# Gate chunks beside the inverse and the scan, latent attention behind the scan

## The chip, the core and the metric

The kernel runs on one core of one Trainium2 chip. The metric is the device time of one execution in microseconds, as a median over runs. The core has five engines that matter here, each with a queue of its own that it works off in order: TensorE (PE, with its weight loads as PEld), VectorE (DVE), ScalarE (ACT), GpSimd (POOL) and SyncE (SP, which issues most DMA transfers).

## What is computed

The reference is one block of a language model on 512 tokens of width 1024, in float32: a two-way RWKV-7 time mix (a scan with a matrix state) and a multi-head latent attention (MLA) side by side, mixed by sigmoid gates, then a mixture of single-neuron experts (PEER), and a gated input of a second kind. The part that the change touches, cut to its core:

```python
h = rmsnorm(x, g_mix)
u = h @ w_in
u_rw, u_mla = u[..., :RW_COLS], u[..., RW_COLS:RW_COLS + MLA_COLS]
gates = sigmoid(u[..., RW_COLS + MLA_COLS:]).reshape(B, T, 2, D)
y_rw = rwkv7_time_mix(u_rw, ...)
y_mla = mla_mix(u_mla, positions, ...)
merged = gates[:, :, 0] * (y_rw @ w_br_rwkv) + gates[:, :, 1] * (y_mla @ w_br_mla)
x = x + merged @ w_out
```

The time mix has 8 heads of 64, in both directions. The attention has 8 heads with 64 plain and 32 rotated (rope) dimensions for q and k, and 64 for v.

## The kernel before

Float32 products are made from two float32r parts: a weight or an input is split into a high and a low part (`whi`, `wlo`; `xh`, `xl`), and each product is three matmuls (`mm3`, L136). A projection chunk of 128 output columns (`uchunk`, L261) is 8 x 3 = 24 matmuls of 512 columns; its weights come by one DMA of 512 KB (`wload`, L121), a copy on ScalarE (L132) and a subtraction on VectorE (L133).

The order of the work is written as Python generators. `drive(main, fill)` (L99) takes a piece of `main`, which says by `yield n` how much filler may stand behind it, and then takes pieces of `fill` until their sum reaches n (in units that are meant as nanoseconds of TensorE). This gives an order of the program; a planner then builds each engine's queue from it, taking the first instruction in this order that is ready by its own estimate of times, so that later work can be pulled into holes where its buffers allow it.

The stages are:

1. `prep` (L335): for each of four pairs of heads c it projects k, r and v (`u_k`, `u_r`, `u_v`), makes decays and rates (`w_a`, for both directions d), normalises k, builds the inputs of the chunked scan (`abkr`), Gram matrices (`gram`) and transposes (`bkt_`, `v_t`), and stores them in memory as packed matrices `pk_d`; 32 pieces of them return as `U`. Beside it, as filler, run `others` (the four chunks of the latent attention's input, the rope tables) and then the first `NG` = 6 of the 16 gate chunks (`gates`, L633; `oth`, L641).
2. `inverse` (L555): 31 steps of forward substitution on VectorE, with two blocks b of 32 x 32 in separate instructions, so that a step is two products and two sums. The result goes to memory (`x_d`, `xt_d`) and comes back as `Xs` and `Xt`.
3. The rest of the gate chunks and the start of the attention stand behind the inverse in the program.
4. `chain` (L652): the scan in 8 steps, with two packed matrices `PK` in the room of `xh` and `xl`, so that it starts when the last gate chunk has read its input. Beside it, as filler, runs the attention.
5. `attn` (L818): values, then for each head `proj_q` and `proj_k`, and for each head and block of 128 queries a score (`score`), a softmax on VectorE and ScalarE, four transposes (`trans`) and the product with v (`pv`). `proj_q` rotates q of each head on 32 partitions on VectorE.
6. The end of `chain` normalises the scan's output (L784 to L811). Then both branches are projected with the gates (`wbr`), and the rest of the kernel follows.

## Time and profile before

| | us |
|---|---|
| median of 3 runs | 1916.23 (1915.2 to 1919.95) |
| the profiled execution | 1914.83 |
| its span | 1912.7 |
| TensorE busy | 1821.6 (95%) |
| VectorE busy | 1540.8 (81%) |
| ScalarE busy | 827.2 (43%) |

A group of instructions is shown as: line, engine, operation, output <- inputs, shape, count | busy us, mean ns of one | idle time of the engine just before them, and what ended it. A row of a timeline begins with the start and the duration in us; "x2" says that two instructions are merged into one row. A row of the chain of waits has the start, the us on the chain, and what it was. Durations of instructions that follow each other overlap a little, so the distance of two starts is the better price. "Clock" is the share of its full speed that TensorE was granted in a stretch.

### The profile page before, as it was taken

How to read it: one execution, taken by the hardware profiler on the slowest of the kernel's cores; microseconds unless marked ns; L12 is line 12 of the kernel's file. 1: busy time of each engine (PE TensorE's matmuls, PEld its weight loads, DVE VectorE, ACT ScalarE, POOL GpSimd, SP SyncE). 2: the span in 40 equal slices, each digit the busy share in tenths (PEclk: the TensorE clock that was granted, in tenths of full speed). 3: DMA queues.
4: the chain of work that ended last, by engine and by line, in shares of the span. 5: the costliest groups of instructions: out<-in, count | busy, mean ns of one | idle time of the engine just before them, and what ended most of it. 6: DMA issues, size and time to landing. Idle time of an engine off the chain costs nothing.

```text
span 1912.7 us, 29780 instructions
## 1 busy us (share of the span) xinstructions
PE 1821.6 (95%) x10969; PEld 1569.8 (82%) x10969; DVE 1540.8 (81%) x3103; ACT 827.2 (43%) x1224; POOL 468.4 (24%) x449
## 2 busy tenths in 40 slices
PE   7999869999999998999999999999999999999997
PEld 6777647777677888999999989888888888888775
DVE  6865778889855889999898965878788788778777
ACT  4755533666334333444444433333333333333354
POOL 1012331220101000332233021334344354344100
PEclk9999989999999999999999999999999999999999
DMA  4355664763434333889999899899999999999862
GB/s 166 90 151 174 165 179 144 226 204 105 149 105 143 100 100 100 260 289 347 339 342 327 307 354 350 315 338 340 338 335 343 322 352 340 340 327 335 280 214 99
DMA packets 196721, 470.19 MB, mean 246 GB/s; under 512 B 33312, under 2 KB 100896, under 8 KB 192736
## 3 DMA queue, kind: packets, MB, share of 16 engines
q1 hardware_dynamic: 146688, 273.23, 43.4%
q0 software_dynamic: 49744, 194.80, 28.7%
q8 instruction: 86, 1.41, 0.3%
q14 instruction: 59, 0.48, 0.1%
q10 hardware_dynamic: 144, 0.26, 0.0%
HBM read 397.97 MB, written 70.25 MB: 245 GB/s over the span
## 4 chain that ended last, share of the span: by engine, by line
PE 69%; DVE 13%; DMA 10%; issue 5%; ACT 3%; POOL 0%; SPq 0%; DVEq 0%; POOLq 0%; ACTq 0%
PE po L1498 20%; PE pa L1150 7%; PE pa L1148 7%; PE pa L1149 7%; DMA row<-in_v,e 6%; PE mm L141 3%; PE mm L142 3%; PE mm L143 3%; DVE wlo L133 2%; PE po L1377 2%; PE q L141 2%; PE q L142 2%; PE q L143 2%; DVE acc L1103 1%; DMA gt<-gates_d 1%
## 5 line engine op out<-in xcount | busy, mean ns | idle before, releaser
L132 ACT ACTIVATE whi<-wraw 128x1024 fp32r<-128x1024 f32 x352 | 370.4, 1058 | 429.7 <-PE pa L1149 157.4
L133 DVE TENSOR_TENSOR wlo<-wraw,whi 128x1024 fp32r<-128x1024 f32 x352 | 428.3, 1221 | 89.6 <-ACT whi L132 82.9
L1150 PE MATMUL pa<-hh,wlo 128*128 128x384 f32 x1024 | 348.9, 341 | 4.3 <-DVE wlo L133 4.3
L1148 PE MATMUL pa<-hh,whi 128*128 128x384 f32 x1024 | 348.9, 341 | 3.5 <-ACT gs L1156 2.5
L1149 PE MATMUL pa<-hl,whi 128*128 128x384 f32 x1024 | 348.3, 340 | 0.0
L1085 POOL DMA_INDIRECT row<-in_u,e x128 | 165.6, 1293 | 423.9 <-DVE row L1093 326.9
L1498 PE MATMUL po<-wlo,wh 128*128 128x512 f32 x768 | 239.1, 392 | 4.3 <-DVE wlo L133 4.3
L1085 POOL DMA_INDIRECT row<-in_v,e x128 | 178.5, 1395 | 248.6 <-DVE acc L1103 234.2
L1498 PE MATMUL po<-whi,wl 128*128 128x512 f32 x768 | 238.4, 392 | 0.0
L1498 PE MATMUL po<-whi,wh 128*128 128x512 f32 x768 | 211.0, 390 | 4.5 <-issue 3.4
L1103 DVE SCALAR_TENSOR_TENSOR acc<-row,pre,acc 128x1024 f32<-128x1024 f32 x127 | 162.7, 1281 | 54.8 <-DMA row<-in_v,e 54.2
L1148 PEld LDWEIGHTS pa<-hh,whi 128*128 128x128 f32 x1024 | 193.2, 189 | 8.2 <-ACT gs L1156 3.2
L1150 PEld LDWEIGHTS pa<-hh,wlo 128*128 128x128 f32 x1024 | 193.0, 189 | 6.6 <-DVE wlo L133 4.6
L1149 PEld LDWEIGHTS pa<-hl,whi 128*128 128x128 f32 x1024 | 193.0, 188 | 3.8
L1498 PEld LDWEIGHTS po<-wlo,wh 128*128 128x128 f32 x768 | 144.6, 189 | 32.4 <-DVE wlo L133 5.1
L1498 PEld LDWEIGHTS po<-whi,wl 128*128 128x128 f32 x768 | 145.3, 189 | 30.9
L1093 DVE SCALAR_TENSOR_TENSOR row<-row,h2t 128x1024 f32<-128x1024 f32 x128 | 155.4, 1220 | 17.5 <-DMA row<-in_u,e 17.4
L1498 PEld LDWEIGHTS po<-whi,wh 128*128 128x128 f32 x768 | 143.0, 188 | 29.4 <-issue 3.6
L147 ACT ACTIVATE wh<-gl 128x384 fp32r<-128x384 f32 x72 | 37.9, 526 | 214.3 <-PE po L1498 214.2
L147 ACT ACTIVATE wh<-ga 128x384 fp32r<-128x384 f32 x48 | 25.2, 524 | 128.2 <-PE po L1498 83.2
L141 PE MATMUL mm<-xh,whi 128*128 128x512 f32 x184 | 74.5, 405 | 4.9 <-ACT gt L637 3.3
L1297 ACT ACTIVATE st<-g 128x512 f32<-128x512 f32 x96 | 50.9, 600 | 54.3 <-PE g L1296 54.3
(465 smaller groups left out, 3178.7 us busy)
## 6 DMA issues: line engine op xcount, KB each, us to landing
wraw<-in_uT SPq DMA_DIRECT2D x128, 512.0 KB
wraw<-in_v SPq DMA_DIRECT2D x128, 512.0 KB
gd<-st POOLq DMA_DIRECT2D x12, 2048.0 KB, 8.2
g<-gd SPq DMA_DIRECT2D x32, 768.0 KB
wraw<-in_w_in SPq DMA_DIRECT2D x35, 512.0 KB
pk<-pk_d SPq DMA_DIRECT2D x16, 1024.0 KB
ga_d<-gs SPq DMA_DIRECT2D x72, 192.0 KB
gl<-ga_d SPq DMA_DIRECT2D x72, 192.0 KB
```

Source lines behind the costliest of these rows:

```text
L132: nc.scalar.activation(hi, raw, AF.Copy)
L133: (nc.gpsimd if s.nw <= NWP else nc.vector).tensor_sub(lo, raw, hi.bitcast(F32))
L141: nc.tensor.matmul(out, hi[:, kw], xh[:, kx], start=(i == 0), stop=False)
L142: nc.tensor.matmul(out, hi[:, kw], xl[:, kx], start=False, stop=False)
L143: nc.tensor.matmul(out, lo[:, kw], xh[:, kx], start=False, stop=(i == n - 1))
L1085: nc.gpsimd.indirect_dma_start(out=r, out_offset=None, in_=table, in_offset=bass.IndirectOffsetOnAxis(ap=e3[:, hk:hk + 1], axis=0))
L1093: nc.vector.scalar_tensor_tensor(r, r, 1.0, h2t, op0=OP.mult, op1=OP.mult, accum_out=pre[:, u:u + 1])
L1103: nc.vector.scalar_tensor_tensor(acc, r, pre[:, u:u + 1], acc, op0=OP.mult, op1=OP.add)
L1148: nc.tensor.matmul(pa, hi[:, k], hh[:, k, 0:NDT], start=(k == 0), stop=False)
L1149: nc.tensor.matmul(pa, hi[:, k], hl[:, k, 0:NDT], start=False, stop=False)
L1150: nc.tensor.matmul(pa, lo[:, k], hh[:, k, 0:NDT], start=False, stop=(k == 7))
L1498: nc.tensor.matmul(po[tb][:, half], w[:, ts], v[:, hs], start=(m == 0 and w is wh and v is vh), stop=(m == 127 and w is wl))
```

## The change

The gate chunks leave the preparation: `oth` is now only `others()`, and one generator `gates(0, 16)` serves as the filler of `inverse` and then of the scan. A gate chunk gives way after every three matmuls (680 units) instead of after the whole chunk, and the preparation gives way only at its start. In `prep` the decays for a direction are made half a turn earlier than they are used. The inverse handles both blocks b in one instruction, and yields after every third step. The scan's packed matrices get a pool of their own (`PKP`), which is released when the scan has ended; only then is the attention's pool `M` made, in part in the same room. The scan's output step is a generator of its own (`chain_out`) with the attention as filler. In the attention the columns of the query weights are laid out anew on the host, so that the rotation is made for four heads at once on 128 partitions (`proj_r`), and its 32 rows for each head are moved by DMA into place; `proj_q` makes two heads at once. `vt` moves into the room of `xh`. The transposes use another PSUM tag (`TC` = 0).

```diff
...
     qi = []
-    for h in range(8):
-        b = h * 96
-        qi += [b + i for i in range(96)] + [b + 80 + i for i in range(16)] + [b + 64 + i for i in range(16)]
+    for g in range(2):
+        bs = [h * 96 for h in range(g * 4, g * 4 + 4)]
+        qi += [b + i for b in bs for i in range(64)] + [b + 64 + i for b in bs for i in range(32)]
+        qi += [b + 64 + (i + 16) % 32 for b in bs for i in range(32)]
     A["wqup"] = c(mla_w_qup[0][:, np.array(qi)].reshape(2, 128, 2, 4, 128).transpose(2, 1, 3, 0, 4)
                   .reshape(2, 128, 8, 128))
...
         yield UNS * 2
         normalise()
         yield UNS * 2
+
+        w_a(0, 0)
         for c in range(4):
             u_k(c)
-            w_a(c, 0)
+            w_a(c, 1)
             u_r(c)
             k_norm(c)
             abkr(c, 0)
-            yield UNS
-            w_a(c, 1)
+            if c < 3:
+                w_a(c + 1, 0)
             if c:
                 gram(c - 1, 1)
                 u_v(c)
...
             if c == 2:
                 shifted(14, lg)
                 nc.scalar.activation(lg, lg, AF.Sigmoid)
-            yield UNS
             if c < 3:
                 gram(c, 0)
-                yield 100
                 bkt_(c, 0)
         gram(3, 0)
         gram(3, 1)
-        yield UNS
         for d in range(2):
             bkt_(3, d)
         v_t(3)
...
 
     def inverse():
 
-        X = [YM.tile([128, 32, 32], F32, name=f"X{b}", tag=f"ym{b}") for b in range(2)]
-        tmp = MU.tile([128, 2, 256], F32, name="xtmp", tag="gt")
+        X = YM.tile([128, 2, 32, 32], F32, name="X", tag="ym")
+        tmp = PKP.tile([128, 2, 256], F32, name="xtmp")
+        nc.gpsimd.memset(X, 0.0)
         for b in range(2):
-            (nc.vector, nc.gpsimd)[b].memset(X[b], 0.0)
+            nc.gpsimd.memset(X[:, b].rearrange("p r c -> p (r c)")[:, ::33], 1.0)
+        for k in range(31, 0, -1):
+
+            w = 32 - k
+            t = tmp[:, :, 0:k * w].rearrange("p b (r c) -> p b r c", r=k)
+            nc.vector.tensor_mul(t, U[:, :, 0:k, k:k + 1].to_broadcast([128, 2, k, w]),
+                                 X[:, :, k:k + 1, k:].to_broadcast([128, 2, k, w]))
+            nc.vector.tensor_add(X[:, :, 0:k, k:], X[:, :, 0:k, k:], t)
+            if k % 3 == 0:
+                yield YI
+        XTt = PKP.tile([128, 32, 32], F32, name="XTt")
+        nc.vector.tensor_copy(XTt, X[:, 0].rearrange("p r c -> p c r"))
         for b in range(2):
-            nc.vector.memset(X[b].rearrange("p r c -> p (r c)")[:, ::33], 1.0)
-        for k in range(31, 0, -1):
-            w = 32 - k
-            t = [tmp[:, b, 0:k * w].rearrange("p (r c) -> p r c", r=k) for b in range(2)]
-            for b in range(2):
-                nc.vector.tensor_mul(t[b], U[:, b, 0:k, k:k + 1].to_broadcast([128, k, w]),
-                                     X[b][:, k:k + 1, k:].to_broadcast([128, k, w]))
-            for b in range(2):
-                nc.vector.tensor_add(X[b][:, 0:k, k:], X[b][:, 0:k, k:], t[b])
-        XTt = M.tile([128, 32, 32], F32, name="XTt", tag="th")
-        nc.vector.tensor_copy(XTt, X[0].rearrange("p r c -> p c r"))
-        for b in range(2):
-            nc.sync.dma_start(x_d[:, b], X[b])
+            nc.sync.dma_start(x_d[:, b], X[:, b])
         nc.sync.dma_start(xt_d, XTt)
 
 
...
 
     def gates(i0, i1, tag="u", pl=None):
         for i in range(i0, i1):
-            ps = uchunk(19 + i, tag, pl)
+            hi, lo = wload(A["w_in"][19 + i], pl)
+            ps = mm_tile(tag=tag)
+            for k in range(8):
+                for w, x in ((hi, xh), (hi, xl), (lo, xh)):
+                    nc.tensor.matmul(ps, w[:, k], x[:, k], start=(k == 0 and w is hi and x is xh), stop=(k == 7 and w is lo))
+                if k < 7:
+                    yield 680
             gt = MU.tile([128, T], F32, name="gt")
             nc.scalar.activation(gt, ps, AF.Sigmoid)
             nc.sync.dma_start(gates_d[i], gt)
-            yield UNS
-
-    oth = itertools.chain(others(), gates(0, NG))
+            yield 680
+
+    oth = others()
     drive(prep(), oth)
     for _ in oth:
         pass
     s.WX.release()
     s.WX = None
     YM = pool(name="ym", bufs=1, side="right")
-    M = pool(name="mla", bufs=2, side="right")
-    GW = pool(name="gw", bufs=2)
+    CH = pool(name="ch", bufs=2)
+    PKP = pool(name="pk", bufs=1)
+    L = {}
 
 
     def chain():
...
         XS = [CH.tile([128, 8, 64], F32, name=f"Xs{i}", bufs=1) for i in range(2)]
         for x in XS:
             nc.gpsimd.memset(x, 0.0)
-        PK = [s.BIG.tile([128, 2, 2048], F32, name=f"pk{i}", tag=("xh", "xl")[i]) for i in range(2)]
+        PK = [PKP.tile([128, 2, 2048], F32, name=f"pk{i}") for i in range(2)]
...
-        L = {}
 
         def load_p(cc, i):
             nc.sync.dma_start(PK[cc % 2][:, i], pk_d[2 * cc + i])
...
+    def chain_out():
+
         g2 = CH.tile([128, 512], F32, name="g2", tag="sw", bufs=1)
         nc.gpsimd.dma_start(g2, A["g2"])
         yield 2000
...
         cql = M.tile([128, 3, T], F32R, name="cql", bufs=1)
         for i in (2, 0, 1):
             split(cqh[:, i], cql[:, i], cqn[:, i])
-        vt = M.tile([128, 4, 8, 2, 64], F32R, name="vt", bufs=1)
+        vt = s.BIG.tile([128, 4, 8, 2, 64], F32R, name="vt", tag="xh")
         for kb in range(4):
             ks = slice(kb * 128, kb * 128 + 128)
             ps = mm_tile(tag="mm")
...
                 nc.tensor.matmul(ps, x[:, 2, ks], flat(w)[:, 512:], start=(i == 0), stop=(i == 2))
             split(vt[:, kb, :, 0], vt[:, kb, :, 1], ps.rearrange("p (h v) -> p h v", h=8))
             yield 650
-        ym = [YM.tile([128, 2, T], F32, name=f"ym{b}", tag=f"ym{b}") for b in range(2)]
-        ymla.extend(ym[c // 2][:, c % 2] for c in range(4))
+        ym = YM.tile([128, 4, T], F32, name="ym", tag="ym")
+        ymla.extend(ym[:, c] for c in range(4))
         KH = [M.tile([128, T], F32R, name=f"kh{i}", bufs=1) for i in range(3)]
         KL = [M.tile([128, T], F32R, name=f"kl{i}", bufs=1) for i in range(3)]
         for i in range(3):
             nc.gpsimd.tensor_copy(KH[i][64:96], krt[64:96])
             nc.gpsimd.tensor_sub(KL[i][64:96], krt[64:96], KH[i][64:96].bitcast(F32))
         sc_ = 96.0 ** -0.5
-        Q, EU, wq, O, TH = {}, {}, [None], [None], [None]
+        Q, RH, EU, wq, O, TH = {}, {}, {}, [None], [None], [None]
+
+        def proj_r(g):
+
+            wq[0] = wload(A["wqup"][g])
+            hi, lo = wq[0]
+            pr = [mm_tile(tag="mm") for _ in range(2)]
+            for i in range(2):
+                mm3(pr[i], hi, lo, cqh, cql, [(4 + i * 2 + k, k) for k in range(2)])
+            rt = M.tile([128, T], F32, name="rt", tag="e", bufs=EB)
+            r2 = M.tile([128, T], F32, name="r2", tag="e", bufs=EB)
+            nc.vector.tensor_mul(rt, pr[0], cosT)
+            nc.vector.tensor_mul(r2, pr[1], sinT)
+            nc.vector.tensor_add(rt, rt, r2)
+            rr = MU.tile([128, 3, T], F32R, name="rr", tag="cqn", bufs=1)
+            split(rr[:, 0], rr[:, 1], rt)
+            RH[g] = rr[:, 0], rr[:, 1]
 
         def proj_q(h):
-            if h % 4 == 0:
-                wq[0] = wload(A["wqup"][h // 4])
+
             hi, lo = wq[0]
             pq = mm_tile(tag="mm")
-            mm3(pq, hi, lo, cqh, cql, [(h % 4 * 2 + k, k) for k in range(2)])
-            qh = M.tile([128, T], F32R, name="qh")
-            ql = M.tile([128, T], F32R, name="ql")
-            rt = M.tile([128, T], F32, name="rt", tag="e", bufs=EB)
-            split(qh[0:64], ql[0:64], pq[0:64])
-            nc.vector.tensor_mul(rt[64:96], pq[64:96], cosT[64:96])
-            nc.vector.tensor_mul(rt[96:128], pq[96:128], sinT[96:128])
-            nc.vector.tensor_add(rt[64:96], rt[64:96], rt[96:128])
-            split(qh[64:96], ql[64:96], rt[64:96])
-            Q[h] = qh, ql
+            mm3(pq, hi, lo, cqh, cql, [(h % 4 // 2 * 2 + k, k) for k in range(2)])
+            for i in range(2):
+                qh = M.tile([128, T], F32R, name="qh", bufs=3)
+                ql = M.tile([128, T], F32R, name="ql", bufs=3)
+                split(qh[0:64], ql[0:64], pq[i * 64:i * 64 + 64])
+                r0 = (h + i) % 4 * 32
+                for x, r in zip((qh, ql), RH[h // 4]):
+                    nc.gpsimd.dma_start(x[64:96], r[r0:r0 + 32])
+                Q[h + i] = qh, ql
 
         def proj_k(h):
             pk = mm_tile(tag="mm")
...
                 nc.scalar.activation(y, O[0][64:128], AF.Copy)
                 nc.vector.tensor_add(y, y, O[0][0:64])
 
+        proj_r(0)
         proj_k(0)
         proj_q(0)
-        yield 1950
-        if PRE:
-            yield -1
+        yield 4700
         for n in range(32 + LP):
             if n < 32:
                 if n % 4 == 1 and n < 28:
                     h = n // 4 + 1
-                    proj_q(h)
-                    yield 1300
+                    if h == 3:
+                        proj_r(1)
+                        yield 2700
                     if h % 2 == 0:
+                        proj_q(h)
                         proj_k(h)
-                        yield 650
+                        yield 2000
                 score(n)
                 yield 650
             if LT_ <= n < 32 + LT_:
...
-    inverse()
+    rest = gates(0, 16, GT)
+    drive(inverse(), rest)
     Oa = R.tile([128, 4, T], F32, name="Oa")
+    drive(chain(), rest)
+    for _ in rest:
+        pass
+    PKP.release()
+    M = pool(name="mla", bufs=2, side="right")
     rest = attn()
-    for _ in gates(NG, NG + GK, GT):
-        pass
-    if PRE:
-        while next(rest) >= 0:
-            pass
-    for _ in gates(NG + GK, 16, GT, GW):
-        pass
-    GW.release()
-    CH = pool(name="ch", bufs=2)
-    drive(chain(), rest, lambda: tc.high_priority(offset=HP) if HP else contextlib.nullcontext())
+    drive(chain_out(), rest)
     for _ in rest:
         pass
     M.release()
...
     return s
 
 
-HP = 0 
-YA = 800
-YB = 800
-YC = 800
-Y0 = 8000
+YA = 1900
+YB = 1900
+YC = 1900
+Y0 = 5000
 ZC = 0
 GQ = 0
 GT = "mm"
 EN = "a"
 NWP = 0
-TC = 99
+TC = 0
 LT_ = 2
 LP = 3
-PRE = 1
-GK = 4
-NG = 6
+YI = 4800
 EB = 3
 NEG = -3.0e38
 GS = 32768.0
```

## Rows read from the trace of the kernel before

**Rows 1.** Length, busy us of PE, PEld, DVE, ACT, POOL; clock, DMA, GB/s.

```profile
58.00:210.00 152.00, 151.10 (x738) 114.97 (x736) 107.59 (x175) 89.70 (x116) 31.18 (x41) 1.00 0.52 142
...
263.00:331.00 68.00, 55.80 (x222) 42.28 (x221) 59.71 (x158) 23.39 (x34) 6.87 (x9) 0.90 0.37 119
...
331.00:345.00 14.00, 9.61 (x67) 6.78 (x65) 10.43 (x22) 9.63 (x18) 6.29 (x12) 0.76 1.05 309
...
345.00:460.00 115.00, 108.24 (x1985) 89.91 (x1985) 104.63 (x207) 74.78 (x146) 20.42 (x37) 0.97 0.60 178
...
460.00:483.00 23.00, 20.92 (x134) 15.21 (x135) 20.51 (x63) 15.34 (x30) 1.07 (x2) 0.93 0.31 105
```

**Rows 2.** Timeline of TensorE: first and last matmul of one gate chunk.

```profile
210.11 0.50 PE L141 MATMUL mm<-xh,whi 128*128 128x512 f32 x1
...
215.56 0.39 PE L143 MATMUL mm<-xh,wlo 128*128 128x512 f32 x1
```

**Rows 3.** Groups by line until 262 us: gate chunks and their table loads.

```profile
L141 PE MATMUL u<-xh,whi 128*128 128x512 f32 x48 | 19.3, 402 | 0.0
...
L637 ACT ACT_TABLE_LOAD x6 | 7.7, 1283 | 0.1
```

**Rows 4.** Chain of waits where the preparation ends.

```profile
252.74 4.46 DMA pk_d<-gm
...
259.26 4.26 DMA U<-pk_d
```

**Rows 5.** Groups by line on VectorE from 262 to 483 us: the inverse.

```profile
L570 DVE TENSOR_TENSOR X<-X,xtmp 128x31 f32<-128x31 f32 (+15 forms) x62 | 21.3, 377 | 0.0
...
L567 DVE TENSOR_TENSOR xtmp<-U,X 128x31 f32<-128x31 f32 (+15 forms) x62 | 20.8, 367 | 6.9 <-DMA U<-pk_d 6.7
```

**Rows 6.** Timeline of VectorE: two steps of the inverse, and its end.

```profile
302.14 0.74 DVE L567 TENSOR_TENSOR xtmp<-U,X 128x252 f32<-128x252 f32 x2
...
302.80 0.75 DVE L570 TENSOR_TENSOR X<-X,xtmp 128x252 f32<-128x252 f32 x2
...
321.49 1.12 DVE L572 COPY XTt<-X 128x1024 f32<-128x1024 f32 x1
```

**Rows 7.** Chain of waits inside the scan: matmul groups of one of its steps.

```profile
394.24 1.08 PE c L729 x32
...
399.07 0.62 PE c L695 x32
```

**Rows 8.** DMA issues: KB each, median us to landing.

```profile
pk_d<-bkt POOLq DMA_DIRECT2D x8, 512.0 KB, 5.1
...
Xt<-xt_d POOLq DMA_DIRECT2D x16, 32.0 KB, 5.7
...
gd<-st POOLq DMA_DIRECT2D x12, 2048.0 KB, 8.2
```

**Rows 9.** Groups by line, 262 to 483 us: attention on ScalarE and VectorE.

```profile
L882 ACT ACTIVATE e<-e,mx 128x512 f32<-128x512 f32 x32 | 22.8, 720 | 14.4 <-DVE mx L880 14.3
...
L879 ACT ACTIVATE e<-s,mx 128x512 f32<-128x512 f32 x32 | 22.0, 686 | 17.7 <-DVE mx L877 11.8 <-PE mm L891 5.0 <-DVE ax L699 0.6
...
L147 ACT ACTIVATE th<-mm 128x512 fp32r<-128x512 f32 x32 | 18.7, 592 | 3.4 <-PE mm L891 3.1
...
L879 ACT ACTIVATION_READ_ACCUMULATOR e<-s,mx 128x1 f32 x32 | 6.2, 195 | 0.0
...
L876 DVE TENSOR_REDUCE mx<-s 128x1 f32<-128x512 f32 x32 | 21.9, 687 | 4.6 <-PE s L874 4.0
...
L148 DVE TENSOR_TENSOR tl<-mm,th 128x512 fp32r<-128x512 f32 x32 | 21.6, 684 | 1.6 <-ACT th L147 1.1
```

**Rows 10.** Timeline of VectorE: last scores of the attention, and its last output.

```profile
463.16 1.39 DVE L876 TENSOR_REDUCE mx<-s 128x1 f32<-128x512 f32 x2
...
468.74 0.68 DVE L876 TENSOR_REDUCE mx<-s 128x1 f32<-128x512 f32 x1
...
482.35 0.68 DVE L916 TENSOR_TENSOR ym<-ym,u 64x512 f32<-64x512 f32 x1
```


## The prediction

> **What bounds the kernel now.** I read the busy time per engine by stretch first, then followed the order of the stages. Until 263 us TensorE runs the preparation of the scan with six of the sixteen gate chunks between its own. From 58 to 210 us it is busy 151.1 of 152 us, VectorE 107.6 and ScalarE 89.7 [rows 1]: the preparation is bound by TensorE there, and every matmul that is taken out of it should come back as time, until VectorE is next. The chain of waits at its end is made of transfers: 4.46 us for a store of the Gram matrices, 4.26 us for loading U, which lands at 263.5 us [rows 4]. The inverse follows on VectorE until 321.5 us [rows 6], with ten gate chunks and the start of the attention beside it; TensorE is not full (55.8 of 68 us) [rows 1]. Then the scan and the attention share all engines: VectorE is busy 104.6 of 115 us between 345 and 460 us [rows 1] and is the bound, so a step of the scan takes 14 us although its matmuls are five groups of 1.08 us and two of 0.62 us, 6.6 us in all [rows 7]. The attention's last output ends at 483.0 us [rows 10]. What lies behind that (projections, routing, experts) is not touched, so I predict the moment of this last output.
>
> **What the change does to each stage.** All times are those of the profiled execution: 1914.83 us, a span of 1912.7 us and 2.1 us around it. It lies 1.4 us under the median of the runs, 1916.23 us.
>
> **The preparation** loses six gate chunks. A chunk is 24 matmuls; their starts run from 210.11 to 215.56 us in 23 steps [rows 2], 0.237 us each, so 5.7 us a chunk and 34 us for six (48 matmuls of each of three kinds [rows 3]). ScalarE also loses six table loads of 1.28 us, 7.7 us [rows 3]. 151.1 less 34 leaves TensorE 117 us for this stretch, still more than VectorE's 107.6 [rows 1], so I take the whole 34 us: U lands at 229 us. Both ends: 220, since the decay products (w_a) now stand half a turn ahead and the table loads they cause leave the last turn (each 1.28 us, and gate chunks at 210 us stood in that turn as well [rows 2, 3]); 246 if only half comes back, because three engines cannot be full at once without a filler. The extra loop order costs no instruction.
>
> **The inverse** goes from 124 instructions to 62 with twice the elements. The old ones sum to 42.1 us [rows 5]. Two of 252 elements start 0.66 us apart, 0.33 us each [rows 6], which is about 0.26 us of elements and 0.07 us of start; over all sizes I take 22.5 us of elements, 62 starts of 0.07 us, and 0.08 us for each product that must now have ended before its sum begins (before, the other half stood between them): 32 us. The ends are 27 and 42 us. Weight subtractions of about 1.2 us for some eight gate chunks stand between them in VectorE's queue: 41 us. The result then goes to memory and back. The trace has no such pair alone; the nearest rows are 5.1 us for a store of 512 KB and 5.7 us for the load of Xt [rows 8], so the scan's first matmul can stand 52 us behind U. The tiles of its inputs no longer wait for the gates' input to come free, so the 14 us of starting up, in which TensorE was busy only 9.6 us [rows 1], are inside this.
>
> **The gate chunks** are now all sixteen beside the inverse and the scan, and they are in front of the scan in TensorE's queue. At 210 us a chunk traced behind the inverse already ran inside the preparation [rows 2]; I count on two of these again. 52 us hold nine more, and 28 us are left. A step of the scan asks three times for 1900 units of filler, which is three groups of 680 units and three matmuls each time: 27 matmuls, 6.4 us, so a step is 6.6 + 6.4 = 13 us. 28 us last 4.4 steps, 57 us. The other 3.6 steps run alone. Their matmuls take 6.6 us, but the second half of the next packed matrix is loaded only half a step ahead: 1 MB, between 5.1 us for 512 KB and 8.2 us for 2 MB [rows 8]. I take 8.3 us a step, 30 us (6.6 and 11 are the ends). Together 52 + 57 + 30 = 139 us; the ends are 126 and 150. A late chunk stops the scan, since the scan's matmuls are queued behind it.
>
> **The attention** follows with the scan's output step beside it. Its buffers need the room of the scan's packed matrices, so none of it can run earlier. A score costs ScalarE 22.8 + 22.0 + 18.7 + 6.2 = 69.7 us for 32, 2.18 us each [rows 9], and three copies of 0.59 us per head of four scores (like the copy of th [rows 9]), 0.44 us: 2.62 us. VectorE's reduction and split are 43.5 us for 32 [rows 9], 1.4 us a score, and with small steps, 0.5 us for projections and 0.6 us for the output step it is about as loaded. So ScalarE sets 84 us. Ahead of the first score stand three splits of 0.6 us, 33 matmuls of 0.237 us, 7.8 us, and the new transfers that carry the rotated rows to each head; nothing in the trace moves SBUF to SBUF, so their price is between nothing and the 5.7 us of Xt [rows 8], and I take 3 us. For later heads three scores cover them. These 16 small transfers go through GpSimd's queue, where only the output step's load of g2 stands. Two products and a sum over 32 rows for each head become the same three over 128 rows for four heads, which is inside VectorE's slack. Behind the last score I take 6 us. 13 + 84 + 6 = 103 us; the ends are 88 (2.2 us a score) and 137 (below).
>
> **The sum.** 229 + 139 + 103 = 471 us against 483 us: 12 us less, 1902.8 us for the profiled execution and, with 1.4 us, 1904 us.
>
> **Rivals.** *Slower: the attention alone waits for itself.* Each score passes from TensorE to VectorE, ScalarE, VectorE, ScalarE, TensorE and back through three buffers. Beside the scan ScalarE sat idle 14.4 + 17.7 + 3.4 = 35.5 us ahead of these steps, 1.1 us a score [rows 9]. If that stays, a score is 3.7 us, the attention 137 us, and the time 1938 us. It decides from 3.0 us a score, (115 - 19) / 32, where the whole gain is gone. For it: the waits name the attention's own steps. Against it: with the scan ending, reductions start from 463.16 to 468.74 us, three intervals in 5.6 us [rows 10], so the pipeline can run at 1.9 us.
>
> *No change: the preparation does not shrink.* Without the filler TensorE waits for VectorE and ScalarE inside each turn, and half of the 34 us stays: 471 + 17 = 488 us, 1921 us. For it: VectorE's 107.6 us is close to TensorE's 117. Against it: the preparation's own chunks can be pulled ahead just as the gates were.
>
> *Much faster: the gates drop into the preparation's holes.* If six chunks and not two run there, the scan has one step with filler and seven alone: 52 + 13 + 58 = 123 us, and with 2.3 us a score, between the 1.9 us of the present end [rows 10] and my 2.62, the attention is 93 us: 445 us, 1878 us. Against it: two accumulation buffers hold the chunks, and one chunk that came early stood in the queue ahead of the preparation's own work.
>
> *The clock falls.* Where TensorE had gaps the granted clock fell: 0.76 with 9.6 busy us of 14, against 0.93 with 20.9 of 23 and 0.97 with 108.2 of 115 [rows 1]. In the attention alone it has 168 matmuls of 512 columns, 40 us at 0.237, and 256 shorter ones that I put at half of that, 30 us: 70 of 103 us. At 0.76 that is 92 us and hides under 103; at half clock it is 140 us, and with some 5 us at its ends the time is about 1946 us. The Trainium skill, "TensorE: Matmul & The Clock Gate", section "A second HAM failure mode: psum-queue depth-cycling", says that short idle times between groups of matmuls make the clock swing between its two levels; by that rule this is where the change would lose. The rows agree that gaps lower it, but show no stretch near half.
>
> **How the numbers follow.** The forecast has a chance of 0.44 (1888 to 1910), the much faster case 0.18, no change 0.18, the slow attention 0.15, the clock 0.05. A measurement of this kernel can tell 0.3%, 5.7 us, so the bounds are 1910.5 and 1922: faster 0.62, same 0.18, slower 0.20. The range runs from 1877 to 1928: below it is half of the much faster case, above it most of the two slow ones.
>
> **What would show it.** U should land between 220 and 246 us, the scan's first step some 52 us later, its steps fall from 13 to about 8.3 us when the gates end, and the scores come 2.6 us apart with ScalarE nearly full. Wrong would be: TensorE idle in the preparation's turns by more than 17 us; gates still running when the scan ends; scores over 3.0 us apart; or scores that run before the scan ends.

## The result and the profile after

The changed kernel takes 1971.95 us (1966.09 to 1974.1), the kernel before 1915.72 in the same series: a ratio of 1.0288 [1.0257, 1.032], slower by 56 us. The forecast was 1904, and the range ended at 1928. The profiled execution has a span of 1969.8 us, 57.1 more than before.

First the stretches, columns as in [rows 1]: length, busy us of PE, PEld, DVE, ACT and POOL, granted clock, DMA share, GB/s. Second half of the preparation, inverse, hand-over to the scan, scan, start of the attention, rest of the attention:

```profile
210.00:260.00 50.00, 50.00 (x271) 39.54 (x270) 28.19 (x38) 15.29 (x22) 14.39 (x21) 1.00 0.76 215
...
273.00:329.00 56.00, 35.72 (x142) 27.95 (x140) 44.72 (x78) 10.14 (x14) 5.11 (x10) 0.84 0.71 230
329.00:342.00 13.00, 4.52 (x100) 4.20 (x102) 1.43 (x4) 0.00 (x0) 3.49 (x6) 0.50 0.52 155
342.00:425.00 83.00, 64.83 (x1669) 59.18 (x1666) 41.82 (x80) 16.89 (x35) 20.46 (x38) 0.82 0.72 209
425.00:452.00 27.00, 19.60 (x67) 14.30 (x65) 20.91 (x51) 10.30 (x17) 8.56 (x10) 0.81 0.13 31
452.00:552.00 100.00, 81.86 (x420) 63.17 (x420) 78.88 (x192) 76.52 (x155) 5.50 (x12) 0.89 0.13 35
```

From the inverse on no stretch fills TensorE: 35.7 of 56, 4.5 of 13, 64.8 of 83, 101.5 of 127 us. Before, the 115 us in which scan and attention stood side by side had TensorE busy 108.2 [rows 1]. The work itself is the same. TensorE's line of the first part of the page (busy us, share of the span, matmuls) says so:

```profile
PE 1841.4 (93%) x10969; PEld 1590.6 (81%) x10969; DVE 1518.4 (77%) x3014; ACT 827.1 (42%) x1223; POOL 473.4 (24%) x467
```

There are 10969 matmuls before and after. TensorE is idle for 1969.8 - 1841.4 = 128.4 us where it was 1912.7 - 1821.6 = 91.1, which is 37.3 of the 57.1 us. The other 19.8 us are the same matmuls taking longer; the granted clock is 0.82 in the scan and 0.50 ahead of it, where the scan before had 0.97 [rows 1].

The gate chunks show where the filler went. First, eighth and last sigmoid of a chunk in the timeline of ScalarE (start, duration):

```profile
200.26 0.60 ACT L644 ACTIVATE gt<-mm 128x512 f32<-128x512 f32 x1
...
259.38 0.58 ACT L644 ACTIVATE gt<-mm 128x512 f32<-128x512 f32 x1
...
315.26 0.58 ACT L644 ACTIVATE gt<-mm 128x512 f32<-128x512 f32 x1
```

Eight chunks run inside the preparation, and all sixteen have ended 22 us before the scan's first matmul, which waits for the inverse's result to come back from memory:

```profile
336.92 1.07 PE L702 MATMUL c<-Xt,pk 32*32 32x32 f32 x32 [22.43 <-DMA Xs<-x_d]
```

So nothing stands beside the scan, and then nothing but the scan's output step beside the attention. The last load of U is issued at 260.5 us (259.3 before), the attention's last output starts at 551.5 (482.35 before [rows 10]). From there to the first maximum of the expert routing it is 125.1 us where it was 134.4: the output step no longer runs in that stretch, and 9 us come back.

### The profile page after: what moved, and what is told of

Read it like the earlier page. It is cut to its first block, busy times and chain, and to the rows that moved or that the text cites. A ratio compares the mean times of both kernels' runs of the same rounds, so it can differ in the third digit from the quotient of the medians.

```text
span 1969.8 us, 29751 instructions
## 1 busy us (share of the span) xinstructions
PE 1841.4 (93%) x10969; PEld 1590.6 (81%) x10969; DVE 1518.4 (77%) x3014; ACT 827.1 (42%) x1223; POOL 473.4 (24%) x467
## 4 chain that ended last, share of the span: by engine, by line
PE 56%; issue 8%; DVE 7%; DMA 4%; ACT 3%; POOL 0%; ACTq 0%; DVEq 0%; POOLq 0%
PE po L1516 26%; PE pa L1166 6%; PE pa L1168 6%; PE pa L1167 6%; PE po L1395 2%; DVE wlo L135 2%; DMA wraw<-in_uT 1%; PE q L143 1%; DVE row L1111 1%; PE q L144 1%; PE q L145 1%; PE g L1314 1%; PE g L1313 1%; PE mm L143 1%; DMA row<-in_u,e 1%
## 5 line engine op out<-in xcount | busy, mean ns | idle before, releaser
L1111 DVE SCALAR_TENSOR_TENSOR row<-row,h2t 128x1024 f32<-128x1024 f32 x128 | 155.8, 1222 | 21.0 <-DMA row<-in_u,e 20.9
L640 PE MATMUL mm<-xh,whi 128*128 128x512 f32 x128 | 52.8, 413 | 5.8 <-ACT gt L644 5.8
## 6 DMA issues: line engine op xcount, KB each, us to landing
gd<-st POOLq DMA_DIRECT2D x12, 2048.0 KB, 10.9
```

The lines of the kernel that those rows point to most:

```text
L640: nc.tensor.matmul(ps, w[:, k], x[:, k], start=(k == 0 and w is hi and x is xh), stop=(k == 7 and w is lo))
L1111: nc.vector.scalar_tensor_tensor(r, r, 1.0, h2t, op0=OP.mult, op1=OP.mult, accum_out=pre[:, u:u + 1])
```

## The experiments

Ratios are against the kernel before in the same series. Stage times are those of each profiled execution.

**Are the gates in the wrong place?** Chunks held behind the preparation's last Gram product, by an order between instructions and with nothing else changed:

```diff
+                    with tc.issue_after(s.hold.ins):
                         nc.tensor.matmul(ps, w[:, k], x[:, k], ...)
```

> The changed kernel, with the matmuls of the gate chunks ordered behind the last Gram matmul of the preparation in TensorE's queue. In the changed kernel eight of the sixteen chunks ran before U landed (at about 265 us). Theory A, the planner pulled them into the preparation and they take its time there: U lands near 230 us, 35 us earlier, the chunks then run beside the inverse and the scan, and the time falls by 25 to 40 us to about 1935-1945. Theory B, the preparation is set by VectorE, ScalarE and its own order: U lands no earlier than 255 us, and since the chunks must still run, the time is 1965 or more.

Measured: 1968.15 us, 1.0278 [1.025, 1.0306]. U's last load is issued at 238.1 us, 22 us earlier, and the gates run from there, most of them 5.6 us apart, up to the scan's first z at 333.4 (z is the first product of a step of the scan). Theory A is right about the chunks and wrong about the time: what leaves the preparation stands behind it. TensorE works through the gates there, busy 88.7 us between 238 and 333, and the scan is as bare as it was.

Next, held once more behind the newest z product of the scan, and with less filler for the inverse, so that 9.5 chunks do stand beside the steps:

> e1 with its gate chunks let out later: a matmul of a chunk may stand only behind the newest z matmul of the scan emitted before it, and the inverse gets 2200 ns of fill per yield where it had 4800. By the program's order 6.5 chunks then stand between preparation and scan and 9.5 beside the eight steps, which is what the prediction meant by 'beside'. Theory 'the planner took the cover away' (the gates ended before the scan, so the scan ran bare): the first z is at about 300 us where e1 had 333, a step takes 13 us (it was 10.3 bare, 8.1 of it PE busy), the last z is at about 395 to 400 where e1 had 414, the last ym near 530, and the time falls by 14 to 20 us against e1, to 1948 to 1955 us. Rival 'gates beside the scan cost what they save': nine chunks of 5.1 us each put about 6 us more into a step, steps are 15 us or more, the last z is at 415 or later and the time stays at 1965 us or more.

Measured: 1978.4 us, 1.0365 [1.0331, 1.0399], the worst of all. The scan's first z is at 311.7, 22 us earlier than in the last run, and its last at 416.5, 2 us later: a step takes 15.0 us with 27 gate matmuls in it, where a bare one took 11.6 in that run. Of their 6.3 us (0.234 us from start to start) 2.9 disappear in the step. The last chunks still ran behind the scan, until 429. The rival's numbers came: this is the arrangement that the prediction had in mind, and it hides less than half of the chunks. But the chunks are also missing where they were taken from. Two stretches of this run, inside the inverse and late in the scan:

```profile
260.00:300.00 40.00, 10.68 (x36) 7.84 (x35) 32.20 (x55) 3.00 (x4) 0.00 (x0) 0.65 0.46 151
...
380.00:420.00 40.00, 38.43 (x671) 31.68 (x671) 21.13 (x37) 7.97 (x11) 3.73 (x7) 0.98 0.56 170
```

From the first z to the last TensorE is idle 6 of 105 us, where it was 22 of 81 in the last run; but ahead of the first z it is idle 36 of 74 us, where it was 6 of 95. Sixteen chunks fill one of the two holes, not both.

**Kernel before, without gates in the preparation** (`NG` = 0, `GK` = 10), and **the changed kernel without gates** (they are set to 0.5 and their projection is left out, 384 matmuls):

> The kernel before, with one thing changed: the six gate chunks leave the preparation's filler and stand behind the inverse in the program (0 instead of 6 beside it, 10 instead of 4 in front of the attention's start). Theory A: the planner pulls several of them forward again, U lands at 255 to 265 us as before, and the time stays within 10 us of 1916. Rival, the forecast's own step: without them the preparation shrinks by 34 us, U lands near 230 us and the time is 1885 to 1900.

> The changed kernel with the sixteen gate chunks left out: the gates are a constant 0.5, stored once per chunk, so that weights, matmuls, splits and sigmoids of the gates are gone. It shows the preparation, the inverse and the scan alone. Theory A: U lands at 225 to 235 us, the inverse takes 35 us instead of 55, the scan 80 to 87 us as in the changed kernel, where the chunks had ended before it began; the time is about 1915. Theory B: U lands at 255 us or later and the time is about 1945.

Measured: 1933.24 us, 1.0086 [1.006, 1.0113], and one time of 1924.03 us. In the first, U's last load is issued at 237.5 us, so its theory A fails, and the rival's time fails too: the preparation shrinks by 22 us and the kernel is slower. In the second U's load is issued at 235.2 us, near theory A, with a time 9 us above it. The two are best read together, from the first instruction of the inverse to the attention's last output. Attention beside the scan: 241 to 505 us. Attention behind the scan: 243 to 509 us. They are as long as each other, though the second does none of the gates. The stretches of the one with gates, by the same columns:

```profile
241.00:291.00 50.00, 45.78 (x184) 36.40 (x183) 47.59 (x136) 14.03 (x19) 7.20 (x6) 0.93 0.36 110
...
370.00:470.00 100.00, 93.35 (x1860) 78.98 (x1856) 90.63 (x182) 65.42 (x131) 19.22 (x35) 1.00 0.61 184
```

and of the one without:

```profile
296.00:385.00 89.00, 63.32 (x1658) 57.99 (x1656) 41.01 (x78) 16.33 (x34) 20.07 (x37) 0.84 0.68 195
385.00:410.00 25.00, 18.96 (x68) 13.55 (x67) 20.26 (x49) 10.55 (x17) 8.99 (x11) 0.86 0.11 19
410.00:510.00 100.00, 80.30 (x421) 60.87 (x422) 80.32 (x197) 76.88 (x158) 6.03 (x12) 0.93 0.14 38
```

Side by side, scan and attention fill TensorE to 93 of 100 us. One after the other, they take 214 us and fill 163. The serial order leaves holes that nothing is there to fill.

**Which waits make the bare scan slow?** Three buffers for its packed matrices instead of two, each loaded three steps ahead:

```diff
-        PK = [PKP.tile([128, 2, 2048], F32, name=f"pk{i}") for i in range(2)]
+        PK = [PKP.tile([128, 2, 2048], F32, name=f"pk{i}") for i in range(3)]
-            if cc < 6:
-                load_p(cc + 2, 0)
+            if cc < 5:
+                load_p(cc + 3, 0)
```

> Only the packed matrices of the scan get three buffers where the changed kernel has two, and a step loads the matrix of three steps on. Theory 'a buffer is free too late': the idle time of PE ahead of the first scan product of the next step (10.0 us over seven steps, released by the packed matrix's DMA in 7.1 of them) goes, a step takes 9 us instead of 10.9, the scan's z go from 76.5 us to 66 to 69, the time is 1962 us. Rival 'the transfers are at their pace' (2 MB a step, DMA share 0.8 beside a bare scan): only one step's load is drawn forward, 2 us go at most and the time stays within 1968 to 1973 us. Rival 'the clock sets the step': the wait for the DMA goes, but z to z stays above 10 us because PE's own matmuls fill the gap.

Measured: 1958.62 us, 1.0252 [1.0219, 1.0285]. Groups by line in the scan (busy us, mean ns | idle before, and what ended it) of the changed kernel:

```profile
L744 PE MATMUL c<-pk,sv 128*64 128x64 f32 x256 | 10.4, 235 | 4.8 <-DVE Oa L781 3.2 <-issue 1.6
L702 PE MATMUL c<-Xt,pk 32*32 32x32 f32 x256 | 7.1, 214 | 32.4 <-DMA Xs<-x_d 22.4 <-DMA pk<-pk_d 7.1 <-DMA yv<-v_d 2.9
```

and with three buffers:

```profile
L746 PE MATMUL c<-pk,sv 128*64 128x64 f32 x256 | 11.7, 249 | 7.7 <-DVE Oa L783 4.0 <-issue 3.7
L702 PE MATMUL c<-Xt,pk 32*32 32x32 f32 x256 | 6.3, 199 | 20.2 <-DMA Xs<-x_d 19.5 <-issue 0.8
```

The 10.0 us of waiting for `pk` and `yv` inside the scan are gone, and 2.9 us come up at the product with `sv`. More comes up elsewhere. The scan with three buffers, to be held against 342:425 of the changed kernel:

```profile
337.00:413.00 76.00, 59.13 (x1662) 53.49 (x1658) 40.41 (x75) 15.57 (x32) 19.27 (x35) 0.91 0.76 201
```

With nearly as many matmuls TensorE is idle 16.9 us where it was 18.2, and busy 59.1 us where it was 64.8, at a clock of 0.91 and not 0.82. So the wait that was mended came back as other waits, and most of the gain is matmuls that take less time. A step falls from 10.9 us to 10.1, not to the 9 that was expected: the theory is right about this one wait, and a step stays over 10 us, as the last rival has it, though other waits and not longer matmuls fill the gap. One execution says little about the size: from the first z to the last it is 70.6 us with three buffers and 76.5 in the changed kernel, but 74.2 to 82.9 over all seven profiled executions with two buffers and nothing beside the scan.

**Where does the inverse lose its start?** In the changed kernel its first product starts 13.0 us after the last load of U is issued (before: 4.1 us). The rows of VectorE and GpSimd:

```profile
273.49 0.27 DVE L567 TENSOR_TENSOR xtmp<-U,X 128x62 f32<-128x62 f32 x1 [5.25 <-ACT whi L134]
```

```profile
273.30 0.99 POOL L665 MEMSET Xs<- 128x512 f32 x2 [4.09 <-DMA v_d<-vtok]
```

The page names ScalarE's weight copy, which ended at 273.29 us. But another tile in memory that the preparation gave back (`Xs`) starts in the same moment, and waits for the preparation's last transfer, v to memory. The change had moved the product tile `xtmp` into such memory. To test it, the tile goes into a free PSUM bank:

```diff
-        tmp = PKP.tile([128, 2, 256], F32, name="xtmp")
+        tmp = mm_tile((128, 2, 256), tag="u")
```

> Only the place of the inverse's product tile: the changed kernel takes it from a pool that stands in the memory the preparation gave back, here it is a free PSUM bank. In the changed kernel the inverse's first product starts at 273.5 us though the last load of U is issued at 260.5; the kernel before needs 4 us for that, this one 13. The first product waits there for U and also for all that last used that memory, the writing out of v (landing at 273.3) among it. Theory 'the tile's place is the new wait': the first product starts at 264 to 266, the transposed copy XTt is at 319 to 322 where it was 328, and the time falls by 5 to 9 us against the changed kernel (which stands at 1.0288 of the kernel before), to a ratio of 1.024 to 1.026. Rival 'gate chunks hold the inverse, wherever it begins' (their weight subtractions stand in DVE's queue and wait for transfers): it begins earlier and ends within 3 us of 328, and the ratio is 1.027 to 1.030.

Measured: 1957.89 us, 1.0235 [1.02, 1.0269]. VectorE's row:

```profile
261.18 0.27 DVE L567 TENSOR_TENSOR u<-U,X 128x62 f32<-128x62 f32 x1 [2.47 <-DMA gates_d<-gt]
```

The inverse starts 3.2 us after the last issue (258.0) and its transposed copy is at 314.2 us instead of 328.1. The theory holds, with more than was expected (10 us of the time).

**Attention.** Deeper buffers (`EB` 5, `LT_` 3, `LP` 4); the output step emitted behind the attention instead of with it; the rotation undone, head by head as before:

> Only depths in the attention loop of the changed kernel: five exponential tiles where there are three, transposes three scores behind instead of two, value products four behind instead of three. Theory 'a score waits for the buffers of the scores before it': 2.9 us per score becomes 2.6, as forecast, the scores take 83 us instead of 91 and the time is 1963 us. Rival 'the four engines together set it' (PE 82 of 100 us busy, DVE 79, ACT 77 in 452:552): 2.8 to 3.0 us per score, the time is within 3 us of 1972.

> Only the order in which the program emits two blocks: latent attention first, then the scan's output step (normalisation and output gate), where the changed kernel drives the output step with attention as its fill. Theory 'the output step stands in the way of attention's start': from the last z to the first score is 31 us in the changed kernel; without the output step ahead it is 18 to 20, the scores end 10 us earlier, and the output step fills holes behind: the time is 1960 to 1964 us. Rival 'attention's start is a chain of its own' (value projection, rotation, splits, copies by DMA): the gap stays at 28 us or more, the output step comes out behind the last score, and the time is 1970 to 1980 us.

> The changed kernel with its rotation of the queries undone: each head projects and rotates its own 32 rows (two products, one sum, a split) where the change rotates four heads at once and copies the rows to their places by DMA. Theory 'the grouped rotation is a gain that attention alone cannot show in full': undone, DVE has 24 instructions of 0.68 us more in the attention block and the scores take 93 to 100 us instead of 91; ratio 1.031 to 1.035. Rival 'the copies by DMA lengthen attention's start': undone, the first score comes 3 to 6 us earlier after the last z (31 us in the changed kernel) and the ratio is 1.025 to 1.028.

Measured: depth 1966.06 us, 1.0277 [1.0237, 1.0317], and the score reductions span 89.7 us where they spanned 90.6: no difference, so the theory of the buffers falls. Order 1967.72 us, 1.0293 [1.0272, 1.0314]: from the last z to the first score it is 26.5 us instead of 31.3, between the two theories, and the scores span 73.3 us, 2.36 us each and not 2.92. But the output step then stands behind, and from the last attention output to the routing it is 147.3 us instead of 125.1. The 22 us are moved, not saved. Scores without the output step, by the same columns as above:

```profile
447.00:521.00 74.00, 62.98 (x349) 50.31 (x350) 60.66 (x145) 66.73 (x139) 4.89 (x10) 0.95 0.11 31
```

Here ScalarE is busy 66.7 of 74 us: that is the bound that the prediction counted on, and it is met only without company. The rotation undone: 1976.15 us, 1.0335 [1.0308, 1.0362], and the scores span 97.7 us. So the grouped rotation is a gain in the serial order, 7 us of the scores' span and about 9 us by the two ratios, whose intervals overlap a little.

**Parts of the change in the kernel before.** The merged inverse alone (its tile where it was before):

> The kernel before with the merged inverse alone: both blocks in one instruction, 62 instead of 124 on VectorE, in the same place. Busy time of the inverse falls from 42 to about 31 us. If VectorE sets the way from U to the scan, the time falls by 5 to 11 us to 1905-1911; if the gate chunks and the start of the attention beside it set it, the time stays within 4 us of 1916.

Measured: 1919.9 us, 1.0027 [1.001, 1.0045], no gain. It runs from 262.7 to 324.7 us, no shorter than with 124 instructions (263.4 to 321.5): its own instructions are busy 35 us instead of 42, but between its steps stands the other work of VectorE's queue. The grouped rotation alone, each head with a projection of its own from half of the columns; then also the earlier decays:

> The kernel before (attention beside the scan, its own preparation and gates) with one part of the change: four heads rotated at once and the rotated rows copied by DMA. Each head still has its own projection (half of the columns of a pair), so that two query tiles do as before. Theory 'DVE sets the stretch where scan and attention stand side by side' (345:460 with DVE busy 104.6 of 115 us): 32 DVE instructions of 0.55 to 0.7 us go and 8 come, some 15 us of DVE time of which about half shows, the last ym is at 474 to 478 where it was 482, and the ratio is 0.995 to 0.998. Rival 'the scan's own steps set it': the last z stays at 456 and the ratio is 0.999 to 1.001. A second rival: the 16 small copies stand behind the scan's loads on GpSimd's queue and make scores wait; ratio above 1.002.

> As the last, and with one more part of the change: the preparation computes a chunk's second decay matrix half a turn earlier (no yields removed, no gate chunk moved). Theory: the preparation is PE bound (151.1 of 152 us busy), so the order within it frees little: U's last load is issued within 2 us of 259 and the ratio equals that of the kernel with the rotation alone within 0.002. Rival: the decays are what the gram products wait for, U is issued 4 us or more earlier and the ratio is 0.003 lower.

Measured: 1916.7 us, 1.0015 [1.0001, 1.003], and 1912.04 us, 0.9996 [0.998, 1.0011]; with the earlier decays U's last load is issued at 258.7 us (259.3 before), as the theory has it. The stretch of scan and attention with the rotation alone:

```profile
345.00:460.00 115.00, 109.35 (x2031) 91.75 (x2030) 90.74 (x189) 69.96 (x139) 26.66 (x50) 0.97 0.70 196
```

VectorE has 13.9 us less to do than in [rows 1], and the last output comes at 481.5 instead of 482.35. The test is not clean. The edit also gives TensorE 24 matmuls more (10993 and not 10969), an estimated 5.7 us at 0.237 us each, and more of the attention's start stands in front of the scan: its first z comes 6.9 us later (355.75 and not 348.85). From there to the last z it is then 97.4 us instead of 107.8. So it cannot tell how much VectorE alone held back. It does show which engine is the fuller one: TensorE is busy 109 of 115 us, and 94.9 of the 97.4 us from the first z to the last, with the end where it was.

**What is left when the waits are mended?** All three together (chunks held, three buffers, tile in PSUM); and against it the same parts with the attention beside the scan again, two buffers in the room of `xh` and `xl`, `NG` = 0, and each head's own projection as in the last runs; and that with six chunks back in the preparation:

> The changed kernel with its mendable waits mended together: gate chunks held behind the preparation (as e1), three buffers for the packed matrices (as x2), the inverse's product tile in PSUM (as x9). Scan and attention still stand one after the other. Theory 'the order itself is the rest': the mends gave 0.1, 0.36 and 0.53 of a hundredth alone, together 0.9 to 1.3, so the ratio is 1.016 to 1.020 and the kernel stays 30 us or more above the kernel before. Rival 'the change loses by its waits': with them gone together, more goes than the sum (they stood one behind the other), and the ratio is 1.008 or less.

> The preparation, inverse (product tile in PSUM), grouped rotation and all sixteen gate chunks behind the preparation as in the change, but latent attention beside the scan as in the kernel before (packed matrices in the space of x, two buffers, gates therefore ended before the scan). Against x10 this undoes the serial order alone. Theory 'the order itself is the rest': ratio 1.000 to 1.006, that is 25 us or more below x10 (e2, which had neither the new inverse nor the rotation, stood at 1.0086). Rival 'gates behind the preparation are the rest': the two differ by less than 10 us.

> As x11, but six gate chunks stand beside the preparation again, as in the kernel before; so it is the kernel before with the change's preparation order, merged inverse (product tile in PSUM) and grouped rotation. Theory 'gates behind the preparation cost, because the preparation has waits that only they fill': the ratio is 0.994 to 1.000, some 6 to 10 us below x11. Rival 'PE bound everywhere, so chunks cost the same wherever they stand': within 4 us of x11.

Measured: 1953.5 us, 1.0213 [1.0179, 1.0247]; 1908.49 us, 0.9976 [0.9959, 0.9993]; 1914.41 us, 1.0 [0.9983, 1.0017]. The first gained a little less than was forecast, the second came out below its range, and the third is 6 us above the second where 6 to 10 us below was expected. In the second run the sixteen chunks are behind the preparation only by the program: the planner pulled eight into it again (U's last load at 260.3), and in the third run it is eight as well, so the third tells nothing of gates and their places. The first and the second differ in the order of scan and attention, and with it in the hold of the chunks (three of which run beside the scan's first steps in the first run), the buffers of the packed matrices and the heads' projections. None of those three gave or cost over 10 us alone. TensorE's line of the page, serial with its waits mended:

```profile
PE 1834.3 (94%) x10969; PEld 1582.9 (81%) x10969; DVE 1520.5 (78%) x3014; ACT 827.7 (42%) x1223; POOL 462.6 (24%) x467
```

and with the attention beside the scan:

```profile
PE 1825.4 (95%) x10993; PEld 1572.3 (82%) x10993; DVE 1517.6 (79%) x3014; ACT 834.6 (44%) x1227; POOL 470.9 (25%) x467
```

Idle: 1950.7 - 1834.3 = 116.4 us against 1911.5 - 1825.4 = 86.1. The serial order costs about 45 us by the medians. The two profiled executions are 39 us apart, of which 30 are TensorE's idle time and 9 its longer matmuls. The mends take 0.75 hundredths off the ratio together and 0.10, 0.36 and 0.53 alone: no larger wait came to light behind them. So of the 60 us between the changed kernel and the one with 0.9976, some 14 go with the mends and 45 with the order. That kernel is the fastest of all here, by 0.24%, with an interval that ends just below 1.

## Why the prediction was wrong

It put the last output at 471 us, and it came at 552. The 81 us, step by step. When its scan started, the forecast had eleven chunks done and five to come; in the run all were done. So five chunks of 5.7 us, 28.5 us, are taken from the one term and from the other. The scan is measured up to the first matmul of its output step.

| step | forecast | measured | off by |
|---|---|---|---|
| scan's first matmul | 281 | 336.9 - 28.5 | 27 |
| scan | 87 - 28.5 | 88.5 | 30 |
| attention: start, scores, end | 13 + 84 + 6 | 24.6 + 91.3 + 10.9 | 24 |

By the forecast's own 8.3 us a step eight bare steps are 66 us, so some 8 of the 30 us are chunks that it had hidden in the steps, and 22 are the steps themselves. All three terms were too small.

**"VectorE is the bound" of scan and attention** is the step that failed first: from it the serial order looked free of cost. The row that was read for VectorE's 104.6 of 115 us has TensorE at 108.2 beside it [rows 1]. The sum of five groups of 1.08 and two of 0.62 us made TensorE look free, but that counted the scan alone. Taking 13.9 us from VectorE there brought the last output forward by 0.8 us, in a run that gave TensorE a little more to do. Where TensorE is at 94%, another order of the same matmuls can win back the other 6% and no more; the prediction never asked how much idle time TensorE would have in the new order. In [rows 1] it was 6.8 and 2.1 us between 345 and 483 us; between 342 and 552 us of the changed kernel it is 18.2, 7.4 and 18.1. The second stretch also holds the attention's start, which stood beside the inverse before; there TensorE was idle 12.2 and 4.4 us [rows 1] and is idle 20.3 and 8.5 now.

**The preparation.** Two chunks were to be pulled into it; it was eight, and U came when it had come before. Of the 34 us, 21 to 24 appeared when the chunks were really kept out (238.1 with the hold, 237.5 with `NG` = 0 and 235.2 without gates, against 259.3), but they are no gain in themselves, because TensorE works off the gates later. That step counted as a gain what was a move.

**The inverse and its hand-over**, 52 us. Its instructions are as cheap as forecast, 32.6 us busy against 32:

```profile
L569 DVE TENSOR_TENSOR X<-X,xtmp 128x62 f32<-128x62 f32 (+15 forms) x31 | 16.3, 527 | 1.0
L567 DVE TENSOR_TENSOR xtmp<-U,X 128x62 f32<-128x62 f32 (+15 forms) x31 | 16.3, 527 | 6.1 <-ACT whi L134 5.2
```

Without gates it runs from 243.2 to 281.5 us, 38 us with some other work between. With them it takes 54.7 us from the first product to the transposed copy where 41 were forecast: VectorE also stands idle 8.6 us in front of the weight subtractions, which wait for ScalarE's copies. Not foreseen either was the wait that the change adds: `xtmp` in memory of the preparation, some 9 us at its start and 14 at its end. TensorE idles 28.8 of the 69 us from 273 to 342, about what this term is off by, but only a part of it goes with `xtmp`: with the tile in PSUM TensorE still idles 20.9 of the 66.6 us from 260 to the scan's first matmul, against 28.2 of 76.9. The prediction spoke of tiles that "no longer wait for the gates' input to come free" and did not ask what the new place waits for. From the transposed copy to the scan's first matmul it is 8.8 us (328.15 to 336.92), inside the 11 us of the forecast.

**The steps of the scan**, 8.3 us bare. Before, a step was 15.4 us from z to z and not 14. The shortest bare steps have the 8.3: z products at 342.20 and 350.75 us. But the others take up to 13.4 us:

```profile
342.20 0.60 ACT L741 ACTIVATE z<-c 128x512 f32<-128x512 f32 x1 [26.36 <-issue]
350.75 0.60 ACT L741 ACTIVATE z<-c 128x512 f32<-128x512 f32 x1 [0.17 <-PE c L736]
364.18 0.60 ACT L741 ACTIVATE z<-c 128x512 f32<-128x512 f32 x1 [0.23 <-PE c L736]
```

The wait for the packed matrix that the prediction named is real and ends in 7.1 us of the idle time; without it a step is still 10.1. The matmuls themselves were taken at the price that they have in company, 6.6 us; bare, they are busy 64.8 us for eight steps, 8.1 each, at a clock of 0.82. A step with 27 gate matmuls was put at 13 us and took 15.0.

**The attention.** A score is 2.36 us without the output step, better than the 2.62 of the forecast, but the output step, put down as 0.6 us a score on VectorE, costs 17 us of the scores' span (90.6 against 73.3). The start was forecast from ScalarE's and TensorE's work as 13 us; in 425:452 VectorE is busy 20.9 of 27 us with splits, the rotation and the output step. The rival "attention waits for itself" came nearer with 1938 us, still 34 us short, and by another cause: with deeper buffers nothing changed.

**The rival "the clock falls"** had a chance of 0.05, and looked for it in the attention. The rows show it lowest in the hand-over and low in the scan as well; how much of the 19.8 us is its doing is not shown. The Trainium skill, "TensorE: Matmul & The Clock Gate", section "A second HAM failure mode: psum-queue depth-cycling", says that short idle times between groups of matmuls make the clock swing; the scan's rows agree (0.82 with 64.8 busy us of 83), and the attention's 0.89 with 81.9 of 100 does so more weakly. Whether the scan would keep 0.97 with the same gaps was not tried.

**The signs of being wrong** did not warn: between 58 and 210 us TensorE is idle 9.4 us and not 17, the gates ended before the scan, the scores are 2.92 us apart and not 3.0, and none ran before the scan ended. Of what should have been seen, U's landing between 220 and 246 us failed first.

**Not settled:** how the 45 us divide between the hand-overs inside a bare step (products wait for VectorE and for each other) and the clock. The nearest is the run with three buffers, whose idle time in the scan is nearly that of the changed kernel (16.9 and 18.2 us) while clock and busy time differ, but it changed the waits too. And the grouped rotation in the layout of the change, two heads from one projection, was not tried beside the scan; it needs a third pair of query tiles.

## What to carry to other kernels

Before two stages that run side by side are put one after the other, add up the idle time of the engine that is busy in both, in the old stretches and in each of the new ones: here, from the inverse to the attention's last output, TensorE was idle 25 of 220 us before and 72 of 279 after, and the mends of single waits gave back only a part. Filler covers one hole at a time: chunks that are moved from one stage to another leave their old place empty. Read the bound of a stretch from all columns of its row, and test it by taking work off the engine that is suspected. A filler that may run early can be pulled early (eight of sixteen chunks here), so what shall stand beside a later stage needs an order that holds it there; and a tile that moves to memory of an earlier stage can wait for what last used that memory, here a transfer out of it.

## What the runs showed of the hardware

The inverse's products went to PSUM at no visible cost: 0.27 us for a product of 62 elements a partition in SBUF and in PSUM, and in the median over all sizes 559 ns in SBUF and 567 in PSUM. In the hand-over to the scan the granted clock was 0.50, the lower of its two levels, 1.2 GHz (4.5 busy us of 13, above), and the 224 matmuls that multiply `yv` with the packed matrix took 278 ns in the mean in the bare scan (clock 0.82) and 251 beside the attention (0.97). With three buffers, bare and at 0.91, it was 238 ns, so the clock alone does not give their price.
